# Weight tiles of a two-layer hybrid encoder: 1 MB transfers into 25 slots, or 2 MB transfers into 12 pairs of slots and one

## The chip, the cores and the metric

One core of one Trainium2 chip. The metric is device time of one execution in microseconds (us). Five engines work at once: TensorE (PE, with its weight loads as PEld), VectorE (DVE), ScalarE (ACT), GpSimd (POOL) and SyncE (SP), which here does nothing but issue transfers; the 16 DMA engines of the core move the data.

## What is computed

Two layers over 256 tokens of width 1024, all in float32, cut to what matters here:

```
for l in 0, 1:
    p = rms_norm(x) @ w_in[l]                         # 1024 x 1440
    y = concat(latent_attention(p), stick_breaking_attention(p), pooling(p))
    x = x + y @ w_out[l]                              # 1024 x 1024
    t = rms_norm(x)
    top-1 of 4 groups, in it top-2 of 8 experts per token
    x = x + sum over 32 experts e: combine[e] * (silu(t @ w_gate[e]) * (t @ w_up[e])) @ w_down[e]
return rms_norm(x)
```

The experts' weights are nearly all of the bytes: 32 experts x 3 matrices of 1024 x 256 floats, 100.7 MB a layer. Each is read once, from HBM, in an order known beforehand.

## The kernel before

**Slots.** On-chip memory has one pool of 25 slots of 128 x 2048 floats (1 MB each). A slot holds either a weight tile that a transfer brings or a work buffer of the kernel (activations split in two, attention scores, the gathered tokens of a group, and so on). The class `Ring` hands them out: `take` (line 82) gives a work buffer, `get` (line 89) returns a weight tile that was loaded, `drop` (line 94) frees. Free slots stand in a queue and the one freed longest ago goes first (line 56).

**The rehearsal.** The program is built twice. The first time nothing is issued: each `take`, `get` and `drop` moves a counter (`tick`, line 59), and the span of ticks in which each name is in use is noted. From these `rehearsed` (line 101) works out the tick at which each weight tile's transfer is issued: the first from which there is a free slot up to its use, by count alone, in the order of `stream`. The second time `tick` issues the transfers at those ticks, all from SP at line 80. SP runs through its own program as fast as it can; each issue waits until the last reader of the slot's former content is done. A semaphore of each transfer is shared by every eighth one, so that an issue also waits until the transfer eight before it has landed.

**Order of the weights.** For each layer: input projection (`wa`, `wqk`, `wvu`), `sm`, `uq`, output projection (`wo` 3, 2, 0, 1), then the experts' tiles `we`. Four experts are one group g of 12 tiles: eight (0 to 7) with gate and up weights, four (8 to 11) with down weights. So `we0` to `we11` are group 0's, `we12` to `we23` group 1's. Groups 0 to 3 are loaded whole; of groups 4 to 7 (`TAIL` = 4) first the eight gate/up tiles of each, then the down tiles by quarter q of the output columns, four per quarter (groups 4, 5, 6, 7), and in layer 0 one tile of the next layer's projection ahead of each quarter. The very last transfer of layer 1 is cut in two halves (`half`, line 70).

**Order of the work.** In a layer: `project_in` (line 352), `mixers` (413, the attentions), `route` (640), `experts` (799). In `experts`, for each g: `hidden(g)` (819) multiplies with tiles 0 to 7, dropping each as it is read; `bend`, `collect(g + 1)` (gathers the next group's tokens into a work buffer `g1`, `g2`, ...), `turn`; and for g < 4 `whole(g)` (850), which reads the four down tiles, drops them together and adds to x. After group 7 come the quarters (`for q in range(4)`): for each of the groups 4 to 7 `down`, a split into high and low parts, `scatter` into the token order; in layer 0 from q = 1 on a part of layer 1's `project_in` between them. An `overflow` branch (940) stands for groups with more than 32 tokens per expert; it takes five slots for a moment and isn't entered here.

**Slots in use in `mixers` and `route`.** Two-slot work buffers are the high and low parts of the same thing: `xH`/`xL`, `wH`/`wL`, `sH`/`sL`, `mH`/`mL`. One-slot buffers are `cw`, `bw`, `vt`, `sp`, `cT`, `kT`, `qT`, `pw`, `x2`, `g0`. At the fullest place (where `mH`, `mL` are taken) eleven slots hold work (`wH`, `wL`, `sH`, `sL`, `mH`, `mL`, `vt`, `sp`, `kT`, `qT`, `pw`) and five the weights `sm` and four `wo`; nine are left for `we`. After it slots come free in this order: `sH` `sL`; `sm`; `wo3`; `sp`; `wo2`; `qT` `kT`; `wo0`; `pw` `vt`; `wo1` (its slot goes to `x2`); `mH` `mL` `wH` `wL` (one of them to `g0`); `x2`. In `experts` there are two more: `hn` and `g1`, taken right after `hidden(0)`.

Of the kernel before, what the change touches and what calls it, by code (L numbers as in the profile page):

```python
# [9 lines left out]
F32 = mybir.dt.float32  # L10
# [12 lines left out]
NSLOT = 25  # L23
AHEAD = 3
NV = 61
TAIL = 4
# [16 lines left out]
class Ring:  # L43
# [4 lines left out]

    def __init__(self, nc, pool, plan):
        self.nc, self.pool, self.plan = nc, pool, plan  # L50
        self.idle = deque(range(NSLOT))
        self.stream, self.issued, self.now, self.cut = [], 0, 0, ()
        self.live, self.first, self.spans = {}, {}, {}

    def tile(self, dtype):
        i = self.idle.popleft()
        return i, self.pool.tile([128, 2048], dtype, name=f"slot{i}", tag=f"slot{i}")

    def tick(self):
        self.now += 1  # L60
        while self.plan and self.issued < len(self.stream) and self.plan[self.issued] <= self.now:
            name, src, then = self.stream[self.issued]
            self.live[name] = i, t = self.tile(F32)
            for i in range(1 if name in self.cut else 2):
                self.half(name, src, i)
            self.issued += 1
            for f in then:
                f()

    def half(self, name, src, i):  # L70

        p, n = src.shape
        t = self.live[name][1][:p, :n]
        if name == self.stream[-1][0]:
# [7 lines left out]
    def take(self, name, dtype=F32):  # L82
        if self.plan:
            self.live[name] = self.tile(dtype)
        self.tick()
        self.first[name] = self.now
        return self.live[name][1] if self.plan else self.pool

    def get(self, name):
        self.tick()  # L90
        self.first.setdefault(name, self.now)
        return self.live[name][1] if self.plan else self.pool

    def drop(self, *names):
        for n in names:
            if self.plan:
                self.idle.append(self.live.pop(n)[0])
            self.spans.setdefault(n, []).append((self.first.pop(n), self.now + 1))
        self.tick()

    def rehearsed(self):

        used = np.zeros(self.now + 3, int)
        for v in self.spans.values():
            for a, b in v:
                used[a:b] += 1
        assert used.max() <= NSLOT, used.max()
        plan, now = [], 1
        for name, _, _ in self.stream:
            use = self.spans[name][0][0]  # L110
            full = np.flatnonzero(used[now:use] >= NSLOT)
            now = min(use, now + full[-1] + 1) if len(full) else now
            used[now:use] += 1
            plan.append(now)
        return plan
# [6 lines left out]
class Net:  # L122
    def __init__(self, tc, ctx, a, plan):
# [17 lines left out]
        def add(name, src, *then):  # L141
            r.stream.append((name, src, then))
# [5 lines left out]
        def we(l, g, *idx):  # L148
            for i in idx:
                add(f"we{g * 12 + i}.{l}", a["we"][(l * 8 + g) * 12 + i])  # L150
# [4 lines left out]
        rest = [lambda i=i: r.half(*r.stream[i][0:2], 1) for i in range(2)]  # L155
# [90 lines left out]
    def weights(self, l):  # L246

        add = lambda name, c, n, last, how=0: self.feed.append((f"{name}.{l}", c, n, last, how))
        for q in range(4):
            for name, n in (("wa", 416), ("wqk", 512)):  # L250
                for k in (2 * q, 2 * q + 1):
                    add(f"{name}{k // 4}", k % 4 * n, n, k % 4 == 3, l + q == 0)
        for k in range(8):
            add(f"wvu{k // 4}", k % 4 * 512, 512, k % 4 == 3)
        add("sm", SM_UK, 512, False, 1)
        add("sm", SM_UV, 512, False, 1)
        for j in range(4):
# [4 lines left out]
        self.wbuf = [v3(self.ring.take(n, F32R), 4, 512) for n in ("wH", "wL")]  # L262
        self.turns = 0
# [56 lines left out]
    def arrive(self, l, q):  # L320

        if q == 0:
            self.xp = [v3(self.ring.take(n, F32R), 8, 256) for n in ("xH", "xL")]
            self.cw = self.ring.take("cw")
            self.weights(l)
# [87 lines left out]
    def mixers(self, l):  # L413
# [63 lines left out]
        ring.drop("xH", "xL")  # L477
# [19 lines left out]
        for j in range(4):  # L497
# [6 lines left out]
            if j == 1:  # L504
                sH, sL = (v3(ring.take(n, F32R), 4, 384) for n in ("sH", "sL"))
# [64 lines left out]
        mixed = [v3(ring.take(n, F32R), 8, 256) for n in ("mH", "mL")]  # L570
# [12 lines left out]
        ring.drop("sH", "sL")  # L583
# [56 lines left out]
    def route(self, l, project):  # L640
# [94 lines left out]
        ring.drop("mH", "mL", "wH", "wL")  # L735
# [63 lines left out]
    def experts(self, l, routed):  # L799
# [66 lines left out]
        weigh(0)  # L866
        for g in range(8):
# [67 lines left out]
        ring.drop("th", "tail")  # L935
        if l + 1 < L:
# [3 lines left out]
    def overflow(self, l, hv, comb, pos, flag):  # L940

        nc, ps, ring, mm = self.nc, self.ps, self.ring, self.mm
        V, A, we = nc.vector, nc.scalar, self.a["we"]
# [8 lines left out]
        with self.tc.If(count > CAP):  # L952
# [6 lines left out]
            with self.tc.For_i(0, 96, 12) as e0:  # L959
                for j in range(4):  # L960
                    for k in range(8):
                        nc.gpsimd.dma_start((g0, g1)[k // 4][:, k % 4 * 512:k % 4 * 512 + 512],
                                            we[bass.ds(e0 + (l * 96 + k), 1), :, j * 512:j * 512 + 512]
                                            .rearrange("o p c -> (o p) c"))
                    for q in range(4):
                        nc.gpsimd.dma_start(dn[:, q * 512:q * 512 + 512],
                                          we[bass.ds(e0 + (l * 96 + 8 + q), 1), :, j * 512:j * 512 + 512]
                                          .rearrange("o p c -> (o p) c"))
                    for t in range(2):
                        for k in range(8):  # L970
                            mm(ps[:, t], hx[:, k, t * 128:t * 128 + 128], v3((g0, g1)[k // 4], 4, 512)[:, k % 4],
                               k == 0, k == 7)
                        A.activation(hd[:, t], ps[:, t, 0:256], AF.Silu)
                        V.scalar_tensor_tensor(hd[:, t], hd[:, t], cw[:, t, j:j + 1], ps[:, t, 256:512],
                                               op0=OP.mult, op1=OP.mult)
                        for c in range(2):
                            self.tr(ps[:, 3, c * 256 + t * 128:c * 256 + t * 128 + 128],
                                    hd[:, t, c * 128:c * 128 + 128])
                    V.tensor_copy(fT, v3(ps[:, 3], 2, 256))
                    for t in range(2):  # L980
                        for n in range(2):
                            for c in range(2):
                                mm(ps[:, 4 + 2 * t + n], fT[:, c, t * 128:t * 128 + 128],
                                   wd[:, 2 * n:2 * n + 2, c], c == 0, c == 1)
                            xs = self.x[:, t, n * 512:n * 512 + 512]
                            V.tensor_tensor(xs, xs, ps[:, 4 + 2 * t + n], op=OP.add)
                V.tensor_copy(tmp[:, :, 0:28], cw[:, :, 4:32])
                V.tensor_copy(cw[:, :, 0:28], tmp[:, :, 0:28])
# [49 lines left out]
def layout(x, norm1_g, w_in, q_norm_g, w_uq, kv_norm_g, w_ukv, pool_w, pool_scale, w_out, norm2_g, w_group,  # L1038
# [24 lines left out]
    gu = gu.transpose(0, 1, 3, 4, 2, 5).reshape(L, 8, 8, 128, 2048)  # L1063
    dn = w_down.reshape(L, 8, 4, 2, 128, 4, 256).transpose(0, 1, 5, 4, 2, 3, 6).reshape(L, 8, 4, 128, 2048)
    o["we"] = np.concatenate([gu, dn], 2).reshape(L * 96, 128, 2048)
# [36 lines left out]
```

## Time and profile before

| | us |
|---|---|
| three runs: median (lowest to highest) | 602.46 (600.61 to 604.20) |
| the profiled execution: its own time | 601.43 |
| its span, first to last instruction | 599.8 |
| mean granted TensorE clock, share of full | 0.959 |
| PE busy / PEld busy / DVE busy | 526.3 / 332.7 / 261.2 |
| moved by the DMA engines | 228.68 MB, mean 381 GB/s |

Busy times are sums over the span; matmuls are pipelined and their ends modelled, so a busy PE isn't one at its peak. Times in the rows are counted from the start of the span. A transfer's time to landing runs from its issue on SP to the semaphore that says that all of it has arrived.

### The profile page before, as it was taken

The numbers are of one execution on the slowest core, as the hardware profiler recorded it, in microseconds if no ns is written. First come the engines' busy times: TensorE is split into PE (matmuls) and PEld (weight loads), VectorE is DVE, ScalarE is ACT, GpSimd is POOL, SyncE is SP. The second block draws the span as 40 slices with busy tenths as digits, with TensorE's granted clock in tenths as the row PEclk, the third lists the DMA queues.
The fourth block names the chain that finished last, engine by engine and source line by source line (L and its number), as shares of the span: only waits on it lengthen the run. The fifth ranks groups of instructions, "written<-read, shape, count | busy, mean of one in ns | idle before, by whom it ended". The sixth has DMA issues, their size and how long they took to land. (4 is left out here: it accounts for less than half of the span.)

```text
span 599.8 us, 10395 instructions
## 1 busy us (share of the span) xinstructions
PE 526.3 (88%) x4168; PEld 332.7 (55%) x4168; DVE 261.2 (44%) x644; ACT 142.7 (24%) x339; POOL 96.6 (16%) x138
## 2 busy tenths in 40 slices
PE   8989999898898688679999899998898868886993
PEld 8959877454354144326667787765344424441562
DVE  5879765432332222215357976662332321221242
ACT  4466453200000000013234854322000000001221
POOL 2535223000000000002113442310000000000011
PEclk9999999989999799959999999998999998997998
DMA  8999777999999999999999958689999999999992
GB/s 300 402 419 413 294 281 306 368 389 423 420 420 422 414 422 422 418 423 417 422 419 421 412 200 325 273 325 392 415 423 421 419 419 421 419 422 423 420 398 89
DMA packets 34619, 228.68 MB, mean 381 GB/s; under 512 B 3841, under 2 KB 6145, under 8 KB 7938
## 3 DMA queue, kind: packets, MB, share of 16 engines
q1 hardware_dynamic: 34130, 227.33, 93.3%
q8 instruction: 36, 0.59, 0.4%
q10 hardware_dynamic: 432, 0.59, 0.3%
q14 instruction: 21, 0.17, 0.1%
HBM read 226.85 MB, written 1.05 MB: 380 GB/s over the span
## 5 line engine op out<-in xcount | busy, mean ns | idle before, releaser
L224 PE MATMUL ps<-slot,slot 128*32 128x256 f32 (+6 forms) x3372 | 406.9, 438 | 53.9 <-DVE slot L780 23.2
L224 PEld LDWEIGHTS ps<-slot,slot 128*32 128x32 f32 (+2 forms) x3372 | 242.8, 143 | 187.2 <-issue 94.6
L242 POOL TENSOR_TENSOR slot<-slot,slot 128x512 fp32r<-128x512 f32 (+1 forms) x38 | 50.9, 1339 | 131.0 <-DVE slot L290 54.6
L288 ACT ACTIVATE slot<-ps 128x256 fp32r<-128x256 f32 (+5 forms) x70 | 33.2, 474 | 142.3 <-PE ps L224 128.4
L833 DVE TENSOR_REDUCE ws<-ps 128x1 f32<-128x256 f32 x16 | 6.8, 425 | 131.1 <-PE ps L282 131.1
L224 PE MATMUL ps<-slot 128*128 128x256 f32 (+3 forms) x224 | 58.8, 406 | 0.0
L830 ACT ACTIVATE slot<-ps 128x256 f32<-128x256 f32 x16 | 6.1, 384 | 209.5 <-PE ps L224 209.5
L809 POOL TENSOR_TENSOR slot<-slot,comb 128x128 f32<-128x128 f32 x32 | 12.2, 401 | 266.0 <-PE ps L224 224.8
L242 DVE TENSOR_TENSOR slot<-slot,slot 128x512 fp32r<-128x512 f32 (+1 forms) x54 | 47.4, 880 | 13.9 <-ACT slot L288 13.5
L224 PEld LDWEIGHTS ps<-slot 128*128 128x128 f32 (+1 forms) x224 | 30.2, 193 | 30.8 <-issue 14.4
L793 DVE TENSOR_TENSOR slot<-ps,vec 128x512 f32<-128x512 f32 x32 | 22.1, 692 | 49.5 <-PE ps L224 49.2
L290 DVE COPY slot<-ps 128x512 f32<-128x512 f32 (+3 forms) x30 | 20.5, 690 | 40.9 <-PE ps L224 32.6
L242 DVE TENSOR_TENSOR slot<-ps,slot 128x256 fp32r<-128x256 f32 (+1 forms) x42 | 18.3, 435 | 43.3 <-ACT slot L288 43.2
L288 ACT ACTIVATE slot<-slot 128x512 fp32r<-128x512 f32 (+1 forms) x54 | 33.0, 613 | 15.8 <-PE ps L224 12.8
L282 PE MATMUL ps<-ident,slot 128*128 128x128 f32 x128 | 24.3, 295 | 5.0 <-DVE slot L835 2.9
L282 PEld LDWEIGHTS ps<-ident,slot 128*128 128x128 f32 x128 | 14.8, 144 | 24.2 <-issue 15.4
L863 DVE TENSOR_TENSOR x<-x,ps 128x512 f32<-128x512 f32 x32 | 22.0, 688 | 8.5 <-PE ps L224 8.2
L224 PE MATMUL ps<-ident,ones 128*128 128x128 f32 x108 | 19.1, 312 | 1.6 <-POOL ident L193 1.6
L244 DVE SCALAR_TENSOR_TENSOR slot<-ps,vec,slot 128x256 fp32r<-128x256 f32 x26 | 12.4, 482 | 17.9 <-ACT slot L288 17.8
L288 ACT ACTIVATE slot<-ps,vec 128x256 fp32r<-128x256 f32 x26 | 12.1, 474 | 27.6 <-PE ps L282 13.2
L290 DVE CAST slot<-slot 128x512 fp32r<-128x512 f32 (+1 forms) x38 | 18.5, 487 | 0.0
L224 PEld LDWEIGHTS ps<-ident,ones 128*128 128x128 f32 x108 | 16.0, 216 | 4.0 <-issue 2.4
(126 smaller groups left out, 303.5 us busy)
## 6 DMA issues: line engine op xcount, KB each, us to landing
slot<-in_we SPq DMA_DIRECT2D x191, 1024.0 KB, 19.6
slot<-in_wo SPq DMA_DIRECT2D x8, 1024.0 KB, 19.2
slot<-in_wvu SPq DMA_DIRECT2D x4, 1024.0 KB, 19.8
slot<-in_wqk SPq DMA_DIRECT2D x3, 1024.0 KB, 19.3
slot<-in_wa SPq DMA_DIRECT2D x3, 832.0 KB, 14.2
slot<-in_uq SPq DMA_DIRECT2D x2, 1024.0 KB, 15.2
slot<-in_small SPq DMA_DIRECT2D x2, 784.0 KB, 15.5
x<-in_x SPq DMA_DIRECT2D x4, 256.0 KB, 6.3
```

The lines of the kernel that those rows point to most:

```text
L224: self.nc.tensor.matmul(out, lhsT, rhs, start=start, stop=stop, skip_group_check=True)
L242: V.tensor_tensor(lo, in_, hi.bitcast(F32), op=OP.subtract)
L244: V.scalar_tensor_tensor(lo, in_, scale, hi.bitcast(F32), op0=OP.mult, op1=OP.subtract)
L282: self.nc.tensor.transpose(out, in_, self.ident)
L288: nc.scalar.activation(out, in_, AF.Copy, scale=1.0 if scale is None else scale)
L290: nc.vector.tensor_copy(out, in_)
L793: self.nc.vector.tensor_tensor(xs[:, 4 * n:4 * n + 4], v3(self.ps[:, b0 + n], 4, 128), self.vec[:, l, 8 + 4 * n:12 + 4 * n, None].to_broad ...
L809: G.tensor_tensor(d4, d4, comb[:, t, 4 * g:4 * g + 4, None].to_broadcast([128, 4, 32]), op=OP.mult)
L830: A.activation(h, ps[:, 2, 0:256], AF.Silu)
L833: V.tensor_reduce(ws, ps[:, 3, 256:512], axis=AX.X, op=OP.add)
L863: V.tensor_tensor(xs, xs, ps[:, 6 + n], op=OP.add)
```

## The change

The 25 slots become 12 pairs of neighbouring slots (128 x 4096 floats) and one single slot. The experts' weights lie in HBM so that two neighbouring tiles of the stream are rows of 16 KB (gate/up tiles 0 and 1, 2 and 3, ...; down tiles 8 and 9, 10 and 11; in the tail groups 4 and 5, and 6 and 7 of one quarter). A stream entry of two names is one transfer of 2 MB where a whole pair is free; half an entry (8 KB rows) may go to a single slot. The last two tiles of layer 1 stay separate entries. The high/low buffers become one work buffer of a whole pair (`two`).

The rehearsal now works out a place for every buffer, tick by tick. Work is seated first (`seat`): a one-slot buffer beside a busy slot if it can, in the slot freed last; a buffer of a pair only in a pair that is wholly free; float32 and float32r never share a pair. Then transfers are placed in stream order: whole pairs first, freed longest ago; else, one tile into a single slot, the single one first, then one with a busy neighbour. A transfer is taken only if all later work can still be seated (`room`). Between the start of the experts' loop and the end of the quarters (`calm`), an entry of two tiles may only go to a whole pair, unless its use is two ticks away or its first tile is already placed.

```diff
-NSLOT = 25
+PAIRS = 12
@@ class Ring
+    def at(self, slot, n, dtype):
+        i = slot // 2
+        if self.hosts.get(i, (None,))[0] != dtype:
+            name, size = (f"pair{i}", 4096) if i < PAIRS else ("one", 2048)
+            self.hosts[i] = dtype, self.pool.tile([128, size], dtype, name=name, tag=name)
+        c = slot % 2 * 2048
+        return self.hosts[i][1][:, c:c + 2048 * n]
@@ tick
+            if len(names) == 2:
+                self.nc.sync.dma_start(t, src[:, us[0] * 2048:us[-1] * 2048 + 2048])
+            else:
+                for i in range(1 if names[0] in self.cut else 2):
+                    self.half(names[0], src, i)
@@ rehearsed
+        def mixed(i, kind, t, ends, kinds):
+            return i < n - 1 and ends[i ^ 1] > t and kinds[i ^ 1] != kind
+        def seat(w, ends, kinds):
+            _, size, kind, a, b = self.works[w]
+            if size == 1:
+                fit = [i for i in range(n) if ends[i] <= a and not mixed(i, kind, a, ends, kinds)]
+                key = lambda i: (kind == F32R and i == n - 1, i < n - 1 and ends[i ^ 1] > a, i == n - 1, ends[i])
+            else:
+                fit = [i for i in whole if max(ends[i:i + 2]) <= a]
+                key = lambda i: max(ends[i:i + 2])
...
+            i = max(fit, key=key)
...
+        def room(t, ends, kinds):
+            ends, kinds, last = list(ends), list(kinds), max(ends)
+            return all(seat(w, ends, kinds) is not None for w in works if t < self.works[w][3] < last)
...
+                if len(spans) == 2 and not part:
+                    tries = [(i, (0, 1)) for i in sorted(whole, key=lambda i: max(ends[i:i + 2]))]
+                if not tries or not sum(c <= t for c in self.calm) % 2 or t + 2 >= spans[0][0]:
+                    tries += [(i, (part,)) for i in sorted(range(n), key=lambda i: (
+                        i < n - 1 and ends[i ^ 1] <= t, i < n - 1, ends[i]))]
...
@@ Net, the stream
-            for g in range(8 - TAIL):
-                we(l, g, *range(12))
-            for g in range(8 - TAIL, 8):
-                we(l, g, *range(8))
+            for g in range(8):
+                for i in range(0, 12 if g < 8 - TAIL else 8, 2):
+                    src = a["wh"][(l * 8 + g) * 4 + i // 2] if i < 8 else a["ww"][(l * 4 + g) * 2 + i // 2 - 4]
+                    add(f"we{g * 12 + i}.{l} we{g * 12 + i + 1}.{l}", src)
...
-                for g in range(8 - TAIL, 8):
-                    we(l, g, 8 + q)
+                for p in range(2):
+                    names = [f"we{g * 12 + 8 + q}.{l}" for g in (4 + 2 * p, 5 + 2 * p)]
+                    src = tails(l, q, p)
+                    if (l, q, p) == (L - 1, 3, 1):
+                        for i in range(2):
+                            add(names[i], src[:, i * 2048:i * 2048 + 2048])
+                    else:
+                        add(" ".join(names), src)
@@ experts
         weigh(0)
+        ring.calm.append(ring.now)
         for g in range(8):
...
         ring.drop("th", "tail")
+        ring.calm.append(ring.now)
```

The body of the branch that isn't entered is rewritten for the new layout of the weights; nothing else of the arithmetic changes.

## Rows read from the trace of the kernel before

**Rows 1.** The page: GB/s in 40 slices of 15 us, and the ending chain by engine.
```profile
GB/s 300 402 419 413 294 281 306 368 389 423 420 420 422 414 422 422 418 423 417 422 419 421 412 200 325 273 325 392 415 423 421 419 419 421 419 422 423 420 398 89
...
PE 25%; DMA 17%; DVE 1%; issue 1%; POOL 0%; ACT 0%; POOLq 0%; ACTq 0%; DVEq 0%; SPq 0%
```

**Rows 2.** Busy us of each engine in chosen stretches, then PEclk, DMA share, GB/s.
```profile
60.00:111.00 51.00, 50.51 (x336) 39.86 (x338) 32.05 (x104) 20.58 (x61) 13.74 (x21) 1.00 0.82 310
111.00:113.00 2.00, 2.00 (x24) 0.55 (x20) 1.62 (x12) 1.18 (x2) 0.00 (x0) 1.00 0.47 86
...
128.00:130.00 2.00, 2.00 (x40) 1.03 (x32) 0.00 (x0) 0.60 (x1) 0.00 (x0) 1.00 0.73 193
130.00:272.00 142.00, 118.15 (x977) 54.53 (x974) 37.22 (x78) 7.30 (x15) 4.56 (x12) 0.93 1.01 420
...
424.00:545.00 121.00, 100.41 (x869) 48.16 (x868) 31.40 (x66) 4.10 (x9) 4.56 (x12) 0.97 1.01 420
```

**Rows 3.** Waits of SP's transfer issues: us in total, times, longest us.
```profile
SPq L80 <- DMA slot<-in_we: 233.0, 117, 3.6
SPq L80 <- PE ps L224: 142.1, 68, 17.6
```

**Rows 4.** PE in time, end of layer 0's experts: start us, us, instruction, idle before.
```profile
257.27 1.93 PE L224 MATMUL ps<-slot,slot 128*32 128x512 f32 x8 [1.41 <-DMA slot<-in_we]
...
261.89 1.93 PE L224 MATMUL ps<-slot,slot 128*32 128x256 f32 x16
264.28 1.93 PE L224 MATMUL ps<-slot,slot 128*32 128x256 f32 x16 [0.46 <-DMA slot<-in_we]
...
274.21 0.37 PEld L224 LDWEIGHTS ps<-slot,slot 128*32 128x32 f32 x12 [0.32 <-DMA slot<-in_we]
```

**Rows 5.** PE in time, end of layer 1's gate/up tiles.
```profile
545.05 1.06 PE L224 MATMUL ps<-slot,slot 128*32 128x512 f32 x8 [1.42 <-DMA slot<-in_we]
...
547.53 1.94 PE L224 MATMUL ps<-slot,slot 128*32 128x512 f32 x8 [1.41 <-DMA slot<-in_we]
```

**Rows 6.** The chain that ended last, in order of time: start us, us, what.
```profile
552.21 37.83 PE ps L224 x384
```

**Rows 7.** Packets in 9 to 11 us (mostly 1 KB rows), and in 430 to 540 us.
```profile
DMA packets 462, 0.79 MB, mean 393 GB/s; under 512 B 32, under 2 KB 347, under 8 KB 462
...
DMA packets 6341, 46.30 MB, mean 421 GB/s; under 512 B 698, under 2 KB 698, under 8 KB 698
```

**Rows 8.** Line 80's weight issues by stretch, first to last start us; us to landing.
```profile
L80 SPq DMA_DIRECT2D slot<-in_we x9: 328/328/328, 22.3 to 42.0; - x9
...
L80 SPq DMA_DIRECT2D slot<-in_we x15: 327/328/1615, 61.9 to 102.8; - x15
...
DMA to landing us min/median/max: 4.8/6.8/10.4
...
L80 SPq DMA_DIRECT2D slot<-in_we x6: 328/328/328, 111.6 to 115.9; - x6
...
L80 SPq DMA_DIRECT2D slot<-in_we x4: 328/330/593, 127.6 to 130.2; - x4
...
DMA to landing us min/median/max: 6.5/8.2/11.4
...
L80 SPq DMA_DIRECT2D slot<-in_we x7: 328/328/328, 134.0 to 139.3; - x7
...
L80 SPq DMA_DIRECT2D slot<-in_we x4: 328/328/693, 417.7 to 420.3; - x4
...
DMA to landing us min/median/max: 6.6/9.1/11.5
...
L80 SPq DMA_DIRECT2D slot<-in_we x7: 328/328/328, 424.1 to 429.4; - x7
```

**Rows 9.** The one issue at line 80 in 257.0 to 257.4 us, and its landing.
```profile
L80 SPq DMA_DIRECT2D slot<-in_we x1: 328/328/328, 257.3 to 257.3; - x1
...
DMA to landing us min/median/max: 19.4/19.4/19.4
```

More of the change, by code (lines that the diff above doesn't have):

```diff
@@ L50, in __init__ @@
         self.nc, self.pool, self.plan = nc, pool, plan
[L51 to L57, printed above, removed]
+        self.stream, self.now, self.cut, self.calm = [], 0, (), []
+        self.works, self.spans, self.live, self.hosts = [], {}, {}, {}
@@ L59, in tick @@
+        self.taken, self.issued = 0, 0
+    def at(self, slot, n, dtype):
[5 more added lines that the diff above has]
+        return self.hosts[i][1][:, c:c + 2048 * n]
     def tick(self):
         self.now += 1
[L61 to L65, printed above, removed]
-            self.issued += 1
-            for f in then:
-                f()
+        while self.plan and self.issued < len(self.plan[1]) and self.plan[1][self.issued][0] <= self.now:
+            _, entry, us, slot = self.plan[1][self.issued]
+            self.issued += 1
+            names, src, then = self.stream[entry]
+            t = self.at(slot, len(us), F32)
+            for u in us:
+                self.live[names[u]] = t[:, (u - us[0]) * 2048:(u - us[0]) * 2048 + 2048]
+            if len(names) == 2:
[3 more added lines that the diff above has]
+                    self.half(names[0], src, i)
+            if us[-1] == len(names) - 1:
+                for f in then:
+                    f()
@@ L80, in half, with take @@
         self.nc.sync.dma_start(t, src)
-    def take(self, name, dtype=F32):
+    def take(self, name, dtype=F32, n=1):
         if self.plan:
-            self.live[name] = self.tile(dtype)
+            self.live[name] = self.at(self.plan[0][self.taken], n, dtype)
+            self.taken += 1
         self.tick()
-        self.first[name] = self.now
-        return self.live[name][1] if self.plan else self.pool
+        if not self.plan:
+            self.works.append([name, n, dtype, self.now, None])
+            return self.pool
+        return self.live[name]
@@ L89, in get, with two @@
+    def two(self, name):
+        t = self.take(name, F32R, 2)
+        return t[:, 0:2048], t[:, 2048:4096]
     def get(self, name):
         self.tick()
-        self.first.setdefault(name, self.now)
-        return self.live[name][1] if self.plan else self.pool
+        self.spans.setdefault(name, [self.now, None])
+        return self.live[name] if self.plan else self.pool
     def drop(self, *names):
         for n in names:
-            if self.plan:
-                self.idle.append(self.live.pop(n)[0])
-            self.spans.setdefault(n, []).append((self.first.pop(n), self.now + 1))
+            if n in self.spans:
+                self.spans[n][1] = self.now + 1
+            else:
+                for w in self.works:
+                    if w[0] == n and w[4] is None:
+                        w[4] = self.now + 1
@@ L99, in drop @@
         self.tick()
     def rehearsed(self):
[L103 to L114, printed above, removed]
@@ L115, in rehearsed @@
-        return plan
+        n = 2 * PAIRS + 1
+        whole = range(0, n - 1, 2)
+        works = sorted(range(len(self.works)), key=lambda w: self.works[w][3])
+        ends, kinds = [0] * n, [F32] * n
+        def mixed(i, kind, t, ends, kinds):
[8 more added lines that the diff above has]
+                key = lambda i: max(ends[i:i + 2])
+            if not fit:
+                return None
+            i = max(fit, key=key)
+            ends[i:i + size], kinds[i:i + size] = [b] * size, [kind] * size
+            return i
@@ L118, in v3 @@
+        return places, plan
 def v3(t, a, b, c0=0):
@@ L261, in weights @@
                 add(f"wo{c // 2}", c % 2 * 1024 + n * 512, 512, c % 2 + n == 2)
-        self.wbuf = [v3(self.ring.take(n, F32R), 4, 512) for n in ("wH", "wL")]
+        self.wbuf = [v3(t, 4, 512) for t in self.ring.two("wHL")]
         self.turns = 0
@@ L322, in arrive @@
         if q == 0:
-            self.xp = [v3(self.ring.take(n, F32R), 8, 256) for n in ("xH", "xL")]
+            self.xp = [v3(t, 8, 256) for t in self.ring.two("xHL")]
             self.cw = self.ring.take("cw")
@@ L476, in mixers @@
         values_in((7,))
-        ring.drop("xH", "xL")
+        ring.drop("xHL")
         for t in range(2):
@@ L504, in mixers @@
             if j == 1:
-                sH, sL = (v3(ring.take(n, F32R), 4, 384) for n in ("sH", "sL"))
+                sH, sL = (v3(t, 4, 384) for t in ring.two("sHL"))
             if j % 2:
@@ L567, in mixers @@
         breaks(0)
-        mixed = [v3(ring.take(n, F32R), 8, 256) for n in ("mH", "mL")]
+        mixed = [v3(t, 8, 256) for t in ring.two("mHL")]
         mH, mL = mixed
@@ L582, in mixers @@
         breaks(2)
-        ring.drop("sH", "sL")
+        ring.drop("sHL")
         normalise(0)
@@ new lines, in row, with onward @@
+            def row(w, i, c):
+                return w[bass.ds(i, 1), :, c:c + 512].rearrange("o p c -> (o p) c")
+            def onward(n):
+                V.tensor_copy(tmp[:, :, 0:32 - n], cw[:, :, n:32])
+                V.tensor_copy(cw[:, :, 0:32 - n], tmp[:, :, 0:32 - n])
+            with self.tc.For_i(0, 4, 1) as g:
+                for j in range(4):
+                    one(j, lambda k, j: row(wh, g * 4 + (l * 32 + k // 2), k % 2 * 2048 + j * 512),
+                        lambda q, j: row(ww, g * 2 + (l * 8 + q // 2), q % 2 * 2048 + j * 512))
+                onward(4)
@@ L989, in overflow @@
+            with self.tc.For_i(0, 2, 1) as p:
+                for i in range(2):
+                    for j in range(4):
+                        one(4 * i + j,
+                            lambda k, _: row(wh, p * 8 + (l * 32 + 16 + i * 4 + k // 2), k % 2 * 2048 + j * 512),
+                            lambda q, _: row(wt, p + (l * 8 + q * 2), i * 2048 + j * 512))
+                onward(8)
         ring.drop(*names)
```

102 lines of the change are left out of this document (62 added, 40 removed).

## The prediction, made before the changed kernel was run

> **What bounds the kernel now.** I read the slices first: 420 GB/s and a little more in most of the span, and less in the first slice, in slices 5 to 9, in 24 to 27 and in the last [rows 1]. So the transfers run at one full rate but for two holes (the attentions of either layer) and the ends. The stretches say it in numbers: 310 GB/s in 60 to 111 us, 86 and 193 in two short dry spells after it, then 420 without a break from 130 to 272; and 420 again from 424 to 545 [rows 2]. In the holes SP waits for matmuls, which is to say for a slot to come free (142 us in all); in the full stretches it waits for the landing eight transfers before (117 times, 233 us) [rows 3]: there slots are to be had and only the rate counts.
>
> What then sets the end? PE has a stock of tiles when the experts begin and eats it faster than it is refilled, so transfers decide only where the stock is gone: at the end of layer 0's experts, where PE waits 1.41 us for each tile, and last at 274.2, for the first tile of quarter 1 [rows 4]; and at the end of layer 1's, where the last gate/up tile is waited for at 547.5 [rows 5]. From there PE works without a gap for 37.8 us [rows 6], and after 274.2 the attentions are PE's own. Two landings thus carry the whole time: what moves the one at 274.2 moves all that follows, and what moves the one at 547.5 against it adds to that. Both hang on streams without slack, so whatever keeps the transfers idle after the last dry spell (130 us; 420 us) is paid in full, and a tile fewer in flight there costs its whole 2.49 us (1.05 MB at 421 GB/s [rows 7]).
>
> **The rate.** A packet is one row, 8 KB now. In two stretches in which the engines are full, 16 engines x 2 us went into 462 packets and 0.786 MB, and 16 x 110 us into 6341 and 46.30 MB [rows 7]. Solved for a cost per packet and one per byte: 0.006 us and 37.2 us per MB. No row of this queue is longer than 8 KB, so 16 KB rows are an extrapolation: a pair loses nine packets per engine of eighteen (eight of data, one for the semaphore), 0.054 us of 4.98. Bounds: nothing (the rows are cut at 8 KB all the same), and 0.11 (the packet's cost were twice as much). I take 0.054, since both stretches support it. The Trainium skill ("DMA: Bandwidth & Descriptors", Anatomy of one DMA and Bandwidth) speaks of a fixed cost of some 2 us per transfer, and of 341 GB/s for 1 MB against 425 for 16 MB. By it 49 pairs in the two full stretches would save about 98 us, an estimate; the trace disagrees, with 1 MB transfers at 421 GB/s already.
>
> **The slots.** I placed the tiles of layer 0 by hand after the diff's rules. At the fullest place nine `we` are loaded (nine issues up to 42.0 us [rows 8]); the planner gets the same nine: `we0` to `we7` in four pairs and, since nine is odd, `we8` alone in the single slot. From there on it is half an entry out of step, and the slots that come free in the attentions come singly (15 issues from 61.9 to 102.8 [rows 8]), which outside the calm stretch are filled singly: `we9` and `we10` in `sH`/`sL`'s pair, `we11` in `sm`'s slot, `we12` to `we19` in those of `wo3`, `sp`, `wo2`, `qT`, `kT`, `wo0`, `pw`, `vt`. So 24 tiles are there when the experts begin, as before; this costs nothing. But their neighbours are not their successors: `we11` sits by `we16` (`qT` was seated beside `sm`), `we14` by `we17`, `we15` by `we18`, `we12` by `we19`. In the calm stretch a slot is of use only with its neighbour:
> - `hidden(0)` frees three pairs for transfers; `hn` and `g1` take the fourth. A pair is free with its second tile: the first issue comes at 112.4 instead of 111.6, one step of 0.86 us later (six issues in 4.3 us [rows 8]). The queue has run dry here, so this is 0.9 us of idle, but contained in what follows.
> - The down tiles freed four slots, at 127.6 to 130.2 [rows 8]. Now only `we9`/`we10` make a pair, at 129.3. On a dry queue 1 MB took 4.8 to 6.5 us from issue to landing [rows 8]; I take 6.5, which is this very spot, and 2.45 for the second MB: it lands at 138.3.
> - The next pair is whole with `we16`, the fifth tile of `hidden(1)`: one step before the last issue at 139.3, so 138.4. Again on a dry queue, it lands at 138.4 + 6.5 + 2.45 = 147.4. The same data landed at 130.2 + 11.4 = 141.6 [rows 8]. **5.8 us lost.** With 4.8 for the latency it is 4.1, with the next partner (`we17`) 6.7. After this whole pairs follow at 139.3, 140.2 and 141.0, each 5 us of data: no idle from here.
>
> Layer 1 I placed in outline: `we9`/`we10` again in `sL`/`sH`'s pair, `we11` again by `we16`. There 428.6 + 6.6 + 2.45 = 437.6 against 420.3 + 11.5 = 431.8 [rows 8]: 5.8 again.
>
> **What a pair does to its reader.** A tile is readable when its pair has landed. In layer 0 the second tile of quarter 1 landed at 257.3 + 19.4 = 276.7 [rows 9], and PE started on the first at 274.2 [rows 4]: 2.5 us later now. (Quarter 0 isn't worse: its pair comes 2.4 us after 261.9 [rows 4], and takes up the wait of 0.46 and what PE then has over before 274.2.) In layer 1 the last two gate/up tiles come together, and PE has two to work through after the landing instead of one: 1.06 us if at the speed of the tile before, 1.94 if at that of the last [rows 5]; I take 1.94. The last two tiles stay single, and the quarters of layer 1 are PE's own with 2 us in hand, so nothing there.
>
> Everything else I cost at nothing. Work buffers taken from the slot freed last could make ACT or DVE wait for PE, but with a ring that full there was hardly a choice of slot before. SP issues fewer transfers and has nothing else to do. The larger branch isn't entered.
>
> **The sum.** Layer 0: 5.8 + 2.5 - 26 pairs x 0.054 (54 transfers lie between the landings at 141.6 and 276.7, two of them single) = +6.9. Layer 1: 5.8 + 1.9 - 23 x 0.054 = +6.5. From 601.43 of the profiled execution, 1 us below the median of the runs, that is **614.8 us**. Its own range is 610.5 (latency 4.8 twice, 1.06) to 618 (no gain in rate, the next partner once).
>
> **The rivals.** A difference under 0.5% (3 us) can't be told from none here.
> - *The freed slots are neighbours.* If my hand placement is wrong and the four down tiles make two pairs, each dry spell grows by 0.9 us only. Layer 0: 0.9 + 2.5 - 1.4 = 2.0; layer 1: 0.9 + 1.1 - 1.2 = 0.8: 604.2, the same within 0.5%. For it: the rules try to seat work beside busy slots, which keeps pairs whole. Against it: the odd ninth tile and the singles after it follow from counts that the issues show. 0.19.
> - *Faster: a fixed cost per transfer shows through the full queue*, and half of the transfers go. A lone one takes 4.8 us where its data take 2.5, so 2.3 are fixed. If a quarter of that (0.58) isn't hidden, 49 pairs save 28 us against 16 of losses (13.4 + 2.6 of rate gain counted there): 589. It decides from 0.39 us a pair on (19 us). Against it: 2.49 - 0.58 would be 550 GB/s, and no slice is above 423 [rows 1]. 0.12, more than that argument leaves it, for what I may have missed. It is the mechanism for which the Trainium skill's page speaks (above).
> - *The change doesn't do what it says*: 16 KB rows go out as packets of 8 KB and the rate stays. 614.8 + 2.6 = 617.4. No row speaks for or against. 0.12.
>
> **Chances.** The forecast 0.57, so slower 0.69, the same 0.19, faster 0.12. Range 603 to 618: it holds the forecast with its bounds, the first and the third rival, and leaves out the second.
>
> **What would show it.** Right: some 80 issues of 2 MB and some 30 of 1 MB; in `hidden(0)` three issues and then one at 129 and none until 137 or later; a dry spell there of 3 us or more, and the like 300 us later; packets of 16 KB at 425 GB/s in the full stretches; PE waits of 2.5 to 3 us for pairs at the ends of the experts; quarter 1 starting near 281 and the last gate/up pair landing near 559. Wrong: two issues of 2 MB between 127 and 131 us, or a full stretch above 435 GB/s.

## The result, and the profile after

The changed kernel took **611.28 us** (median of 4 runs, 610.59 to 612.18) against 602.29 of the kernel before beside it: ratio 1.0147, 95% interval 1.0110 to 1.0183, so 9 us slower. The forecast was 614.8 with a range of 603 to 618. The profiled execution took 611.73 us (before: 601.43), its span 610.1, at a mean granted TensorE clock of 0.963.

The page of the changed kernel: GB/s in 40 slices of 15 us, packets, the queue of the weights, the ending chain by engine, and the costliest issues.

```profile
GB/s 297 400 426 390 300 270 322 348 345 334 428 426 426 421 428 426 425 429 425 426 416 425 387 61 358 292 324 373 315 429 429 428 424 425 424 428 428 426 411 102
DMA packets 22957, 228.70 MB, mean 375 GB/s; under 512 B 2545, under 2 KB 4849, under 8 KB 6642
...
DMA 11%; PE 5%; issue 1%; DVE 0%; ACT 0%; POOL 0%; POOLq 0%; ACTq 0%; DVEq 0%; SPq 0%
...
pair<-in_wh SPq DMA_DIRECT2D x56, 2048.0 KB, 26.8
pair<-in_wt SPq DMA_DIRECT2D x15, 2048.0 KB, 34.3
pair<-in_ww SPq DMA_DIRECT2D x10, 2048.0 KB, 12.1
pair<-in_wh SPq DMA_DIRECT2D x15, 1024.0 KB, 7.1
pair<-in_ww SPq DMA_DIRECT2D x11, 1024.0 KB, 8.1
```

81 issues carry 2 MB. Against [rows 1] the full slices went from about 420 to about 426 GB/s, and the holes became deeper: the tenth slice (137 to 152 us) from 423 to 334, and the twenty-ninth (427 to 442 us) from 415 to 315. The change pays in the first and costs in the second. The same by stretch: us of each engine, then PEclk, DMA share, GB/s.

```profile
111.00:113.00 2.00, 2.00 (x21) 0.68 (x24) 1.59 (x8) 0.61 (x2) 0.00 (x0) 1.00 0.56 238
...
130.00:142.00 12.00, 11.91 (x90) 3.50 (x78) 3.50 (x6) 0.38 (x1) 0.00 (x0) 1.00 0.66 218
142.00:272.00 130.00, 99.77 (x856) 48.58 (x857) 32.76 (x70) 5.90 (x12) 4.53 (x12) 0.95 1.01 426
...
445.00:555.00 110.00, 88.72 (x767) 42.58 (x768) 28.38 (x59) 3.71 (x8) 4.41 (x12) 0.95 1.01 427
```

In 130 to 142 us, where before the full stretch had already begun [rows 2], the engines now move 218 GB/s with TensorE busy throughout: the weights wait, not the reader yet. What they wait for stands in SP's waits (us in total, times, longest), to be held against [rows 3]:

```profile
SPq L75 <- PE ps L303: 282.5, 65, 37.5
SPq L75 <- DMA pair<-in_wh: 48.7, 12, 5.4
SPq L93 <- DMA pair<-in_wt: 41.1, 9, 5.2
```

Waiting for matmuls, which is for a slot to come free, rose from 142 us to 282; the waits for an earlier landing fell from 233 to about 100, of which 90 in the two groups shown. (With half as many transfers eight of them are twice as many bytes, so part of this only changes its name.) The issues of pairs in four stretches of the two layers, the last three with their time to landing:

```profile
L75 SPq DMA_DIRECT2D pair<-in_wh x3: 328/328/392, 113.0 to 116.4; - x3
...
L75 SPq DMA_DIRECT2D pair<-in_wh x1: 328/328/328, 129.9 to 129.9; - x1
...
DMA to landing us min/median/max: 9.1/9.1/9.1
...
L75 SPq DMA_DIRECT2D pair<-in_ww x1: 327/327/327, 139.0 to 139.0; - x1
...
DMA to landing us min/median/max: 8.3/8.3/8.3
...
L75 SPq DMA_DIRECT2D pair<-in_ww x1: 328/328/328, 435.8 to 435.8; - x1
...
DMA to landing us min/median/max: 8.8/8.8/8.8
```

Three issues after `hidden(0)`, one at 129.9, the next at 139.0: where the kernel before filled four slots from 127.6 to 130.2 [rows 8], one pair goes out, and nothing else for nine microseconds. The data of 139.0 landed at 147.3; before, they landed at 141.5. TensorE's waits for weights at the ends of the two layers (start us, us, instruction, idle before), to be read beside [rows 4, 5]:

```profile
255.97 1.92 PE L303 MATMUL ps<-pair,pair 128*32 128x512 f32 x16 [3.06 <-DMA pair<-in_wh]
...
261.71 3.24 PE L303 MATMUL ps<-pair,pair 128*32 128x512 f32 x16 [3.82 <-DMA pair<-in_wh]
...
281.50 1.93 PE L303 MATMUL ps<-pair,pair 128*32 128x256 f32 x16 [2.64 <-DMA pair<-in_wt]
553.85 3.01 PE L303 MATMUL ps<-pair,pair 128*32 128x512 f32 x16 [1.98 <-DMA pair<-in_wh]
558.65 3.25 PE L303 MATMUL ps<-pair,pair 128*32 128x512 f32 x16 [1.79 <-DMA pair<-in_wh]
```

Quarter 1 of layer 0 starts at 281.50 instead of 274.21 [rows 4], the last gate/up tiles at 558.65 instead of 547.53 [rows 5]. After that the chain, in order of time, holds a new row where before TensorE alone stood [rows 6]:

```profile
558.67 34.22 DMA pair<-in_wt
592.88 0.04 issue
592.93 8.41 PE ps L303 x92
```

The quarters of layer 1 now touch the landings too, though lightly: TensorE's two longest waits for a tile in them are 0.55 and 0.70 us.

### The profile page after: what moved, and what is told of

Its sections match the earlier page's. It is cut to its first block, busy times and chain, and to the rows that moved or that the text cites. A ratio compares the mean times of both kernels' runs of the same rounds, so it can differ in the third digit from the quotient of the medians.

```text
span 610.1 us, 10216 instructions
## 1 busy us (share of the span) xinstructions
PE 522.6 (86%) x4168; PEld 331.8 (54%) x4168; DVE 260.9 (43%) x644; ACT 142.9 (23%) x339; POOL 95.3 (16%) x138
## 5 line engine op out<-in xcount | busy, mean ns | idle before, releaser
L303 PE MATMUL ps<-pair,pair 128*32 128x256 f32 (+5 forms) x3028 | 358.4, 434 | 43.3 <-DVE pair L859 13.3
L303 PEld LDWEIGHTS ps<-pair,pair 128*32 128x32 f32 (+1 forms) x3028 | 214.3, 140 | 158.9 <-issue 81.1
L303 PE MATMUL ps<-pair 128*128 128x128 f32 (+4 forms) x352 | 75.4, 364 | 6.8 <-DVE pair L859 6.7
L367 ACT ACTIVATE pair<-ps 128x256 fp32r<-128x256 f32 (+5 forms) x70 | 33.2, 474 | 142.3 <-PE ps L303 128.7
L303 PEld LDWEIGHTS ps<-pair 128*128 128x128 f32 (+1 forms) x352 | 45.8, 196 | 37.8 <-issue 12.8
L321 POOL TENSOR_TENSOR pair<-pair,pair 128x512 fp32r<-128x512 f32 (+1 forms) x33 | 44.4, 1346 | 85.7 <-DVE pair L369 50.6
L321 DVE TENSOR_TENSOR pair<-pair,pair 128x512 fp32r<-128x512 f32 (+1 forms) x47 | 41.4, 882 | 15.1 <-ACT pair L367 14.7
L369 DVE COPY pair<-ps 128x512 f32<-128x512 f32 (+3 forms) x30 | 20.5, 690 | 41.2 <-PE ps L303 33.0
L367 ACT ACTIVATE pair<-pair 128x512 fp32r<-128x512 f32 (+1 forms) x47 | 29.0, 619 | 15.4 <-PE ps L303 9.9
L361 PE MATMUL ps<-ident,pair 128*128 128x128 f32 x120 | 21.7, 286 | 5.0 <-DVE pair L914 2.9
```

Source lines behind the costliest of these rows:

```text
L303: self.nc.tensor.matmul(out, lhsT, rhs, start=start, stop=stop, skip_group_check=True)
L321: V.tensor_tensor(lo, in_, hi.bitcast(F32), op=OP.subtract)
L361: self.nc.tensor.transpose(out, in_, self.ident)
L367: nc.scalar.activation(out, in_, AF.Copy, scale=1.0 if scale is None else scale)
L369: nc.vector.tensor_copy(out, in_)
```

## The experiments

The theory: the time was lost because in the calm stretch a slot is of use only with its neighbour, which leaves the transfers idle behind the first groups of either layer; the long rows win back a part. The rivals: the loss is that two tiles land as one (their reader waits), or 2 MB transfers themselves cost something. Results first; the first four ran on one chip beside 13 runs of the kernel before (median 601.55), the last four on another beside 11 (602.13), so across the two groups, and with the change (beside four runs, 602.29), the ratios are to be compared. Their intervals leave a difference of two ratios uncertain by 0.3 to 0.5%, which is 2 to 3 us.

| run | median us | ratio to before, 95% |
|---|---|---|
| the change | 611.28 | 1.0147 (1.0110 to 1.0183) |
| calm stretch begins at group 2 | 602.66 | 1.0010 (0.9991 to 1.0029) |
| each pair as two transfers | 612.59 | 1.0174 (1.0142 to 1.0207) |
| two transfers only where read at once | 609.58 | 1.0147 (1.0121 to 1.0172) |
| 2 MB transfers of 8 KB rows | 615.54 | 1.0230 (1.0204 to 1.0255) |
| later calm and two transfers | 597.95 | 0.9929 (0.9910 to 0.9949) |
| the same, no pairs in layer 0's hole | 597.17 | 0.9915 (0.9890 to 0.9939) |
| pairs alone, no halves early | 608.85 | 1.0109 (1.0082 to 1.0135) |
| later calm in layer 1 alone | 608.28 | 1.0102 (1.0077 to 1.0127) |

**Later calm.** The slots that the first groups free may be filled singly:

```
         weigh(0)
-        ring.calm.append(ring.now)
         for g in range(8):
+            if g == 2:
+                ring.calm.append(ring.now)
```

> Half entries into single slots stay allowed until group 2 begins, so that slots freed by groups 0 and 1 are refilled whether or not their neighbour is free. Slots theory (the time went into slots that stood empty beside a neighbour still in use): six issues of 1 MB between 112 and 117 us as in the kernel before, the idle of the transfer engines at 136 to 140 us goes, layer 0 and layer 1 gain some 3 to 4 us each; 604.5 us (603 to 607). Landing theory (the time went into two tiles landing as one, the empty slots were hidden): no change, 611.3 (610 to 612.5).

602.66 us, just below the range of 603 to 607: 8.2 us of the loss are gone (1.0147 - 1.0010 of 602). 130 to 142 us of this kernel:

```profile
130.00:142.00 12.00, 12.00 (x90) 3.63 (x82) 3.44 (x5) 0.23 (x1) 0.00 (x0) 1.00 0.92 355
```

355 GB/s instead of 218, with long rows everywhere else (426 and 427 in the two full stretches). The slots theory holds; the rival that the landing of two tiles as one is the loss had forecast no change. The pair at 130.1 still comes alone, on a queue that has run dry, and lands 9.4 us later.

But the 8.2 us are not all slots of the transfers. Held against the change instruction by instruction, TensorE in this execution is 3.6 us earlier at 290 us, 6.5 at 350 and 9.3 at its end. The 2.9 us between 290 and 350 are gained in layer 1's attentions, which don't wait for weights. There ScalarE waits for GpSimd in the change, as it did before (3.23 us), and doesn't here (first the change, then this run):

```profile
335.48 0.84 ACT L367 ACTIVATE pair<-ps,vec 128x256 fp32r<-128x256 f32 x2 [3.22 <-POOL pair L321]
```

```profile
329.12 0.84 ACT L367 ACTIVATE pair<-ps,vec 128x256 fp32r<-128x256 f32 x2 [0.32 <-PE ps L361]
```

The edit moves the work buffers too. What ScalarE writes in this row is `cT`; the rehearsal seats it, in the change, in the slot of the weight tile `wvu0.1`, which GpSimd is still reading, and here in the slot that `cw` has left. TensorE gains some 1.7 us by it also against the kernel before, and another 1.2 against the change, since the latter's stretch at the lower clock there (343 to 348 us, shown below) doesn't come. No run has the one without the other. So, by this trace, some 6 of the 8.2 us belong to the transfers. The wait is also gone in three of the runs below: both together, no pairs in layer 0's hole, and pairs alone.

**Later calm in one layer.**

```
-        ring.calm.append(ring.now)
+        if l == 0:
+            ring.calm.append(ring.now)
         for g in range(8):
+            if l == 1 and g == 2:
+                ring.calm.append(ring.now)
```

> Only layer 1 gets the later beginning of the stretch in which pairs wait; layer 0 stays as in the changed kernel. The changed kernel took 611.3 and the one with both layers later 602.7. If each layer loses the same, as the prediction had it (5.8 us each): 607.0. If layer 1 loses less, because there the next pair of slots is whole at its third tile and not at its fifth (the pair landed 2.9 us late in all, against 5.8): 608.5.

608.28: layer 1's share is 0.45% or 2.7 us, what the edit does in layer 0 the rest of the 8.2, 5.5. That fits the second of the two expectations; by their intervals (2.7 and 1.9 us either way) the times alone don't exclude equal shares. And ScalarE's wait stands in this run, so of the 5.5 us the 2.9 in layer 1's attentions come from other seats, and 3.6 were gained by the end of layer 0 in the trace of the run with both layers later.

**Two transfers of 1 MB for a pair**, in the same places: rows of 8 KB again, and each tile readable by itself.

```
-                self.nc.sync.dma_start(t, src[:, us[0] * 2048:us[-1] * 2048 + 2048])
+                for j, u in enumerate(us):
+                    self.nc.sync.dma_start(t[:, j * 2048:j * 2048 + 2048], src[:, u * 2048:u * 2048 + 2048])
```

> Places and plan as in the changed kernel, but each pair is issued as two transfers of 1 MB with rows of 8 KB. Slots theory: the rate falls back from 428 to 421 GB/s, which costs 49 pairs x 0.073 = 3.6 us; each tile is readable when it has landed, which gives back 2.5 us at quarter 1 of layer 0 and 1 to 2 us at the last gate/up tile of layer 1; the dry spells stay: 610.8 us (609 to 612.5). Landing theory: most of the 9 us comes back, 605 or less. If the long rows gave nothing, 607.

**2 MB transfers with 8 KB rows**: the two tiles of a pair lie one behind the other in HBM, and one transfer fetches both.

```
-                self.nc.sync.dma_start(t, src[:, us[0] * 2048:us[-1] * 2048 + 2048])
+                self.nc.sync.dma_start(t.rearrange("p (e n) -> p e n", e=len(us)),
+                                       src[us[0]:us[-1] + 1].rearrange("e p n -> p e n"))
...
```

> The pairs lie in HBM as two tiles, so that one transfer of 2 MB consists of rows of 8 KB; places, plan and number of transfers as in the changed kernel. If the gain in rate comes from the longer rows: 421 to 423 GB/s in the full stretches, 49 pairs x 0.066 = 3.2 us more, 614.5 us (613.5 to 616). If it comes from the larger transfer (fewer semaphores and issues): 428 GB/s still, 611.3.

The three belong together. The full stretches of the second and the first (as the windows above):

```profile
142.00:272.00 130.00, 99.15 (x843) 47.84 (x847) 31.95 (x68) 5.51 (x11) 4.54 (x12) 0.94 1.01 420
445.00:555.00 110.00, 91.23 (x776) 45.82 (x774) 29.06 (x60) 3.71 (x8) 4.54 (x12) 0.94 1.01 420
```

```profile
142.00:272.00 130.00, 103.17 (x854) 49.23 (x854) 32.37 (x69) 5.76 (x11) 4.56 (x12) 0.90 1.01 421
445.00:555.00 110.00, 87.87 (x768) 41.21 (x768) 27.34 (x57) 3.71 (x8) 3.80 (x10) 0.97 1.01 421
```

Transfers of 2 MB with short rows run at 420 GB/s, those of 1 MB at 421 here and at 420 before [rows 2], and only long rows at 426. So the rate comes from the row and not from the size of the transfer, and halving the number of transfers is worth nothing to a full queue. In time, long rows are worth 0.83% (1.0230 - 1.0147, some 5 us, 2.7 either way; 615.54 is in the range for it). That two tiles land as one costs 2.9 us (615.54 - 612.59, same chip; 2.5 either way), so cutting all pairs in two loses about as much in rate as it gains at the reader, and ends no better than the change (612.59, just above its range of 609 to 612.5).

**Two transfers only where the reader waits**: the last gate/up pair of either layer and the down tiles of the last groups.

```
-                self.nc.sync.dma_start(t, src[:, us[0] * 2048:us[-1] * 2048 + 2048])
+                cut = names[0].split(".")[0] in ("we56", "we57", "we58", "we59", "we80", "we81", "we82", "we83", "we90")
+                for c in [[u] for u in us] if cut else [us]:
+                    n = (c[0] - us[0]) * 2048
+                    self.nc.sync.dma_start(t[:, n:n + 2048 * len(c)], src[:, c[0] * 2048:c[-1] * 2048 + 2048])
```

> Only the pairs whose first tile is waited for (the last gate/up pair of group 7 and the down pairs of groups 4 to 7, in both layers) are issued as two transfers of 1 MB. Slots theory: quarter 1 of layer 0 starts 2.4 us earlier, the last gate/up pair of layer 1 costs one tile of PE less behind the landing (0.9 to 1.7 us), the cut pairs lose 0.073 us each, of which some ten count: 607.5 us (606 to 609.5). Landing theory: the whole 9 us, 603. If a landing of two tiles costs nothing: 611.9.

609.58: just above the theory's range (606 to 609.5), 1.7 us under the change by the medians and no gain by the ratio (1.0147 for both, 2.7 us either way), so the time leaves open whether the cut alone gains. The profiled execution is the shortest of five, 607.02 (the others took 609.19 to 610.75). TensorE in it, and its clock in two stretches of this kernel and then of the changed one:

```profile
261.52 1.94 PE L306 MATMUL ps<-pair,pair 128*32 128x512 f32 x8 [2.47 <-DMA pair<-in_wh]
278.48 2.55 PE L306 MATMUL ps<-pair,pair 128*32 128x256 f32 x22
281.36 1.07 PE L306 MATMUL ps<-pair,pair 128*32 128x256 f32 x16 [0.33 <-DMA pair<-in_wt]
```

```profile
265.00:270.00 5.00, 4.02 (x34) 1.51 (x34) 1.31 (x4) 0.59 (x2) 0.00 (x0) 0.50 1.02 423
270.00:275.00 5.00, 5.00 (x40) 2.75 (x36) 0.85 (x2) 0.77 (x2) 0.00 (x0) 0.55 1.01 419
```

```profile
265.00:270.00 5.00, 2.19 (x20) 1.16 (x24) 1.67 (x4) 1.67 (x2) 0.00 (x0) 0.78 1.00 428
270.00:275.00 5.00, 4.09 (x48) 2.21 (x39) 0.93 (x3) 1.15 (x3) 0.00 (x0) 0.88 1.01 426
```

Here the cut did what it was meant to do: quarter 1 starts at 278.48 without a wait, where the change waited 2.64 us and started at 281.50, and what is left is a wait of 0.33 for its second tile. The execution is 4.7 us shorter than the profiled one of the change. That is so although TensorE was at its lower level (0.50 and 0.55, that is 1.2 GHz nearly throughout) from 265 to 275 us, where the change had 0.78 and 0.88. Why the other four executions took 2 to 4 us longer isn't shown; they have no trace, and their mean granted clocks (0.943 to 0.962) lie below this one's 0.964.

**Both together.**

> Both edits together: the stretch in which pairs wait for neighbouring slots begins at the third group of the experts, and the pair read first in layer 0's quarter 1 of the down tiles, the last gate/up pair of layer 1 and the down pairs of the last groups go out as two transfers. If the loss in the slots and the loss at the readers are two separate terms of a sum, this is 602.7 of the first edit alone less the 1.7 of the second alone: 601.0 (range 599.5 to 602). If the second edit gained only because the first spell had made everything late, 602.7 stays. The gain of the long rows (0.073 us a pair, 81 pairs) would leave it 1 us or so under the kernel before, which is less than 0.5%.

597.95, 3 us under the forecast and below its range, and faster than either kernel: on top of the later calm the cut is worth 0.81% or 4.9 us (1.0010 - 0.9929, 1.6 either way). Alone it was worth nothing by the ratio and 4.7 us in the one traced execution, so whether the two are terms of one sum stays open. Where it acts it shows: quarter 1 of layer 0 starts at 275.66, with the later calm alone at 278.07. TensorE's waits before quarter 1 of layer 0 and for the last gate/up tile of layer 1, which in the change ended at 281.50 and 558.65:

```profile
275.66 4.97 PE L306 MATMUL ps<-pair,pair 128*32 128x256 f32 x38 [1.15 <-DMA pair<-in_wt]
...
547.18 1.06 PE L306 MATMUL ps<-pair,pair 128*32 128x512 f32 x8 [1.42 <-DMA pair<-in_wh]
```

The last gate/up tile starts 0.35 us earlier than before the change [rows 5], though quarter 1 of layer 0 is 1.45 late [rows 4]; this execution was 1.49 late at 100 us already. Of what it has gained since, 1.7 us are ScalarE's wait in layer 1's attentions, which is gone here.

**No pairs in layer 0's hole.** In addition, from the experts' start to group 2 of layer 0 every tile goes alone (`slow` holds the two ticks):

```
...
-                if len(spans) == 2 and not part:
+                if len(spans) == 2 and not part and not sum(c <= t for c in self.slow) % 2:
...
```

> As the run before it in this list, but in layer 0 no pair at all is formed from the experts' start to the third group, so that the four slots that the down tiles free are each filled at once with 1 MB, as in the kernel before. Slots theory: the second spell of layer 0 shrinks by another 1 to 1.6 us and 99.5 of every 100 bytes still go in long rows elsewhere; 599.5 (598 to 601), the fastest of all kernels here. Rival, by which the spell that is left no longer bounds (something other than the landing of quarter 1 sets layer 0's end): the same as the run before it in this list, within 0.5 us.

597.17, the fastest here and below its range of 598 to 601, but 0.8 us from the run before it is within the intervals. The spell itself is gone, and with it the wait before quarter 1 (no row of it in this trace):

```profile
128.00:130.00 2.00, 2.00 (x44) 1.23 (x40) 0.00 (x0) 0.60 (x1) 0.00 (x0) 1.00 1.03 434
130.00:142.00 12.00, 11.99 (x90) 3.57 (x82) 3.44 (x5) 0.31 (x1) 0.00 (x0) 1.00 1.01 419
```

So the profile answers to the theory, and the time can't tell it from the rival.

**Pairs alone.** The planner may not load half a pair before it is due, so that every tile lies beside its successor, at the price of two tiles fewer in stock:

```
-                if not tries or not sum(c <= t for c in self.calm) % 2 or t + 2 >= spans[0][0]:
+                if not tries or t + 2 >= spans[0][0]:
```

> Half a pair is loaded only where the tile is due at once: the attentions' slots are filled by pairs or not at all, so 22 tiles instead of 24 are in stock when the experts begin, but each sits beside its successor, so that pairs of slots come free together afterwards. If what costs is that neighbours in the slots are not neighbours in the stream: 609.5 (607.5 to 611), two tiles fewer in stock being made up by the spells that vanish. If what costs is the stock at the start and the bytes that are late, two tiles fewer are 4.9 us a layer on top: 616 to 621.

608.85, in the range of the slots theory (607.5 to 611) and far below the 616 of the other. Three stretches:

```profile
60.00:111.00 51.00, 50.52 (x340) 40.16 (x340) 32.09 (x111) 21.80 (x65) 14.59 (x22) 1.00 0.67 271
111.00:113.00 2.00, 2.00 (x20) 1.41 (x23) 1.34 (x3) 0.00 (x0) 0.00 (x0) 1.00 0.96 410
...
130.00:142.00 12.00, 11.59 (x82) 3.37 (x74) 3.81 (x6) 0.38 (x1) 0.00 (x0) 1.00 1.01 431
```

The dry spells are gone (410 and 431 GB/s); what is lost is the transfers ahead of the experts (271 GB/s where before 310 [rows 2]: 2 MB). That the total fits is in part luck: ScalarE's wait is gone here too. In the traces TensorE is 1.0 us later than in the change at 290 us, and 2.0 earlier at 350. Whole pairs everywhere, and singles in the attentions with whole pairs after them, are thus two ways to lose, 2.3 us apart by the ratios, which is within their intervals; filling singly until the holes are past loses less than either.

## Why the prediction came out right, point by point

The forecast's case came true: slower, in the range, 3.5 us under the value, and by the mechanism that it named, as the later calm showed. That the total came so near is in part luck: terms that the sum didn't have cancel in large part. Against the profiled execution of before, TensorE's timeline gives the sum step by step (the same instruction in both traces; predicted +13.4, measured +10.3 in own time).

- *The slots* (5.8 us in layer 0): the hand placement was right, which rules out the rival of four neighbouring slots. The issues came at 113.0 (forecast 112.4), 129.9 (129.3) and 139.0 (138.4), all 0.6 late, since the first landings of the execution were 0.6 later; the pair landed at 147.3 (147.4). Latency of a pair on a dry queue, taken as 6.5 + 2.45 = 8.95 from a single's row: 9.1 and 8.3. So the landing was met by two errors of 0.6 us that cancel, and 5.2 of the 5.8 us are the slots' own.
- *Layer 1, "5.8 again"*: mis-sized. TensorE was 8.1 us late when it had done the first group's gate/up tiles, and the first pair of `hidden(1)`'s slots landed 12.75 late (444.6 against 431.8): 4.7 lost. The outline was one tile off: by the rehearsed places `we11` sits by `we15` there, the fourth tile, and not by the fifth (nor by the third, as the expectation to the run with layer 1 alone has it). After the gain in rate that leaves 3.0 at the last landing (forecast 4.6), which the 2.7 of the run with layer 1 alone fit.
- *The rate* (0.054 us a pair, up to 0.11): 0.073. In the full stretches pairs land 4.895 us apart (median) where two tiles took 2 x 2.484. The rival of 8 KB packets is out by the packets on the weights' queue (packets, MB, share of 16 engines), first of the change and then of the run with 8 KB rows:

```profile
q1 hardware_dynamic: 22466, 227.33, 91.0%
```

```profile
q1 hardware_dynamic: 32834, 227.33, 91.1%
```

- *The fixed cost per transfer* as a rival (589): wrong. The Trainium skill ("DMA: Bandwidth & Descriptors", Anatomy of one DMA) puts some 2 us of fixed cost on a transfer, by a fit to transfers that GpSimd issues; here SyncE issues them. The trace shows more on a dry queue (8.3 to 9.1 us for 4.9 us of data), and none that fewer transfers would save in a full one: 420 GB/s with 2 MB transfers and 421 with 1 MB.
- *The reader in layer 0* (+2.5): TensorE waits 2.64 before quarter 1, which starts 7.3 late; 0.65 of it came from the start, so 6.65 for a forecast of 6.9. Taken away by the cut, it moved the start of quarter 1 by 3.0 us in the traced execution (278.48), and by 2.4 on top of the later calm (275.66 against 278.07); only in the second case did the time follow clear of noise.
- *The reader in layer 1* (+1.94): two tiles after the landing took 1.3 more. But the tail got 2.7 back, which no step had: in the eleven microseconds behind the last landing the clock was at 0.54 before and is at 0.85 after (first before, then after):

```profile
547.00:558.00 11.00, 9.03 (x56) 3.88 (x56) 2.50 (x6) 2.44 (x4) 0.00 (x0) 0.54 1.01 420
```

```profile
558.00:569.00 11.00, 8.37 (x76) 3.73 (x80) 2.52 (x6) 2.43 (x4) 0.00 (x0) 0.85 1.01 429
```

- *What the sum lacked altogether* is this clock. Between 281.5 and 362 TensorE lost another 2.4 us in two stretches at its lower level (1.2 GHz), in the parts where it is itself the bound (before, the same work ran at 1.00). In layer 1's first group it got 1.6 back, since the kernel before was at 0.66 in 411 to 415, and the changed one at 1.00 in the same work (the last row is of before):

```profile
281.00:286.00 5.00, 4.50 (x34) 2.70 (x38) 2.28 (x6) 0.90 (x2) 1.18 (x1) 0.66 0.98 412
343.00:348.00 5.00, 5.00 (x19) 4.03 (x19) 3.79 (x6) 3.37 (x6) 2.54 (x4) 0.67 0.99 418
416.00:422.00 6.00, 4.26 (x38) 2.72 (x30) 1.85 (x6) 2.46 (x3) 0.00 (x0) 1.00 1.02 434
```

```profile
411.00:415.00 4.00, 4.00 (x26) 4.00 (x26) 0.69 (x1) 0.00 (x0) 0.00 (x0) 0.66 1.02 428
```

Put together: 0.65 + 6.65 + 2.4 - 1.6 = 8.1, + 3.0 + 1.3 - 2.7 = 9.7, + 1.6 in the quarters of layer 1, where TensorE waits for tiles again, and 1.0 less between TensorE's end and that of the span: 10.3. Of the 3.1 us by which the forecast of the sum was too high, layer 1's landing makes 1.6 and the two readers' terms 0.9; the terms that the sum didn't have, each up to 2.7 us, come to 0.6 in the kernel's favour. The terms of the clock were read from traces and not tried. The work buffers' seats, which the prediction named and put at nothing, did cost nothing against the kernel before, since ScalarE's wait stands in both; what they can cost showed only in the experiments.

## What to carry to other kernels

A coarser transfer is only as good as the slots: where buffers come free one by one, a rule that waits for neighbours turns each hole in the stream into a longer one, and on a stream without slack that is paid in full (some 6 of the 8.2 us here, against 5 won by the rows). Form large transfers where the queue is full anyway, fill singly where it runs dry, and split again where a reader waits for the last tile: the same change so bounded made 597 us of 602, of which 1.7 us are another buffer's seat. A planner seats every buffer anew when one of its rules is edited: before a gain is put down to the rule, look along the whole timeline for where it arises.

## What the runs showed of the hardware that was not expected

- Row length shows in a full queue, transfer size doesn't: 426 to 427 GB/s with 16 KB rows, 420 with 8 KB rows in transfers of 2 MB, 420 to 421 in transfers of 1 MB.
- TensorE's lower clock level stood behind stretches in which it waited (0.66 in 281 to 286, after a wait of 2.64 us; 0.50 in 265 to 270 of the run with cuts, after one of 2.47), and by then TensorE may be the bound. It doesn't stand behind every wait: after the same wait for GpSimd in layer 1's attentions (1.22 and 1.23 us) the clock was 1.00 before (333 to 338) and 0.67 in the change (343 to 348). Time and clock go together in much of the spread: of the thirteen runs of the kernel before beside the first four experiments, the one with 0.951 of the full clock took 604.37 us, the one with 0.966 599.79; but two with 0.959 took 601.25 and 603.67, and which of the two causes the other isn't shown.
